# A hybrid encoder layer on one core: the second norm's scale and shift move to the transposed blocks and to the last stage's residual rows, and the inputs' low parts move to VectorE

## The chip, the cores and the metric

The kernel runs on one core of one Trainium2 chip. Time is device time in microseconds of that core. Three runs of the kernel before gave 1482.79, 1483.11 and 1485.83 us; the median, 1483.11 us, is the figure to compare with. Five engines work side by side, each through its own instructions in a fixed order: TensorE (PE), VectorE (DVE), ScalarE (ACT), GpSimd (POOL) and SyncE (SP), which here only issues DMAs. An instruction that waits holds back everything behind it on its engine.

## The reference, cut to what matters

```
h = LN(x, ln0_g, ln0_b)                      # 1024 positions x 1024 channels, float32
p = h @ w_in                                 # four mixers: S5, RWKV-7, short conv, Fourier
y = concat(y_a, y_b, y_c, y_d)
h = LN(alpha*h + y @ w_out, ln1_g, ln1_b)    # the "second norm"
f = (silu(h @ w1) * (h @ w3)) @ w2           # hidden width 2816
out = LN(alpha*h + f, ln2_g, ln2_b)          # alpha = 2**0.25
LN(x, g, b) = (x - mean) * rsqrt(var + 1e-5) * g + b
```

The result of the second norm is used twice: as the input of the two hidden products, and, times alpha, as the residual under the last norm.

## The kernel before

Positions stand in 8 tiles of 128 rows. Every matmul operand in full precision is split into a high part (a cast to fp32r, "hi") and a low part (the value less its high part, "lo"), and each product is three matmuls (`mm3`, L158 to L162). A split is one ACT cast and one subtraction on POOL or on DVE (`split_to`, L1382 to L1385).

The order of the instructions on each engine is set by a scheduler that lays the program out on a simulated clock, with the priorities that the code gives, so the program's text alone doesn't give the order. The stages that the change touches:

**The output projection** (about 640 to 800 us of the profile, beside the end of the RWKV scan at first and the start of the hidden products at last). The tiles go from 7 down to 0. For each tile:
- `residual` (L1428) loads the rows of x, recomputes the first norm from its kept mean and reciprocal deviation `st0` (DVE, L1432), multiplies by alpha times the first norm's scale (POOL, L1434) and adds alpha times its shift (DVE, L1435). The scale and shift rows are spread over the 128 partitions in the tile `rows`.
- `out_load` (L1437) loads the mixers' output `yraw` and splits it: the cast on ACT, the low part on DVE for tiles 7 and 6, on POOL for tiles 5 to 0 (the last argument in L1441).
- `out_product` (L1446) makes two halves of 24 matmuls, each in a PSUM bank `ops`; two banks of that kind (tag `pj`) take turns. DVE adds each half to the residual (L1455), which is also what gives the bank back to PE.
- `norm` (L1462) takes mean and variance (L172 to L187) and applies them with the scale and shift rows `g1`, `b1` in two DVE instructions of 128x1024 with two tensor inputs each (L1465, L1466).
- `turn` (L1507), once for every two tiles, transposes the normed rows on PE into PSUM (`ot`, L1518), copies each group of four 128x128 blocks to SBUF with one ACT copy (L1519), multiplies the rows by alpha (ACT, L1520), writes them to DRAM as `d_acc` (L1521), and makes seven sums and differences of the blocks `hb` on DVE (L1528 to L1535), each split into the hidden products' operands `H` (the products are done by a 2x2 scheme with seven products in place of eight).

**The hidden products** (`ff_hidden`, L1597) run from about 780 to 1273 us, with weights split on the way.

**The last product** (`ff_second`, L1668) has seven products n = 0 to 6 of 11 steps, about 31 us each. The left operands `fa` come back from DRAM; the right ones `fb` are made of `w2` tiles, by a sum on DVE (L1725), a cast on ACT and a low part on DVE, in a ring of six buffers, four steps ahead. Four PSUM banks are added to the rows `acc` when a product ends (L1761). After product 3 the residual rows are read back from `d_acc` through a ring of two buffers `fx` (L1779) and added on DVE (L1780). The last norm (`ff_out`, L1801) is applied by ACT, POOL and DVE with the rows `g2`, `b2` (`b2` lies in the tile `rmask`), loaded once by ACT's DMA queue at L1678 and L1679.

Of the kernel before, what the change touches and what calls it, by code (L numbers as in the profile page):

```python
# [12 lines left out]
F32 = mybir.dt.float32  # L13
# [10 lines left out]
NT = S // 128  # L24
# [12 lines left out]
for _name, _cols in (  # L37
    ("ln0_g", 8), ("ln0_b", 8), ("mu_rkv", 12), ("w0", 4), ("a0", 4), ("k_k", 2), ("k_a", 2),
    ("r_k", 2), ("gn_g", 2), ("gn_b", 2), ("conv_w", 6), ("glu_b", 2), ("mu_w", 16), ("mu_a", 16),
    ("mu_g", 8), ("lam_re", 16), ("lam_im", 16), ("log_dt", 16),  # L40
):
    VEC[_name] = (_n, _cols)
    _n += _cols
# [3 lines left out]
def pack(inp):  # L47
# [9 lines left out]
        col(a["rwkv_mu_w"][0]), col(a["rwkv_mu_a"][0]), col(a["rwkv_mu_g"][0]),  # L57
        s5(a["s5_lambda_re"]), s5(a["s5_lambda_im"]), np.repeat(a["s5_log_dt"][0], 64, axis=0),
    ], axis=1)
    rows = np.stack([a["ln0_g"], a["ln0_b"], a["ln1_g"][0], a["ln1_b"][0], a["ln2_g"][0], a["ln2_b"][0]])  # L60
# [79 lines left out]
class Trunk:  # L140
# [1264 lines left out]
    def row_load(self, out, i):  # L1405
        self.nc.scalar.dma_start(out=out, in_=self.A["rows"][i:i + 1, :].to_broadcast([128, D]))


    def out_first(self):
        nc = self.nc  # L1410
        rows = self.t("TT", [128, 4, D], "rows")
        self.row4 = [rows[:, i] for i in range(4)]
        for i in range(4):
            self.row_load(rows[:, i], i)
        for i in range(2):
            nc.scalar.mul(out=rows[:, i], in_=rows[:, i], mul=ALPHA)
        self.acc = [None] * NT
# [10 lines left out]
    def residual(self, t, tag):  # L1428
        nc = self.nc
        ht = self.acc[t] = self.t(tag, [128, D], "acc")  # L1430
        nc.sync.dma_start(out=ht, in_=self.A["x"][t * 128:(t + 1) * 128, :])
        nc.vector.tensor_scalar(out=ht, in0=ht, scalar1=self.st0[:, t, 0:1], scalar2=self.st0[:, t, 1:2],  # L1432
                                op0=ALU.subtract, op1=ALU.mult)
        nc.gpsimd.tensor_tensor(out=ht, in0=ht, in1=self.row4[0], op=ALU.mult)  # L1434
        nc.vector.tensor_tensor(out=ht, in0=ht, in1=self.row4[1], op=ALU.add)  # L1435

    def out_load(self, t):  # L1437
        nc = self.nc
        raw = self.raw("yraw").rearrange("p (k s) -> p k s", k=8)
        nc.sync.dma_start(out=raw, in_=self.d_y[:, :, t * 128:(t + 1) * 128].rearrange("k p s -> p k s"))  # L1440
        self.split_to(*self.y_parts(t), raw, nc.vector if t > 5 else None)  # L1441

# [14 lines left out]
    def out_proj(self):  # L1457
        nc = self.nc
        g1, b1 = self.row4[2:]
        self.raws = ["WR", "T7"]  # L1460

        def norm(t):  # L1462
            ht = self.acc[t]
            mean, rstd = self.row_stats(self.m, ht, D, LN_EPS)
            nc.vector.scalar_tensor_tensor(out=ht, in0=ht, scalar=mean, in1=g1, op0=ALU.subtract, op1=ALU.mult)  # L1465
            nc.vector.scalar_tensor_tensor(out=ht, in0=ht, scalar=rstd, in1=b1, op0=ALU.mult, op1=ALU.add)  # L1466

# [39 lines left out]
    def turn(self, j, tags):  # L1507
# [4 lines left out]
        for t, dst in ((7 - 2 * j, (b11, b21)), (6 - 2 * j, (b12, b22))):  # L1512
            ht = self.acc[t]
            for q in range(2):
                ps = self.ps("fs", [128, 4, 128], "ot")
                for k in range(4):
                    kt = 4 * q + k
                    nc.tensor.transpose(ps[:, k, :], ht[:, kt * 128:(kt + 1) * 128], self.ident)  # L1518
                nc.scalar.copy(out=dst[q], in_=ps)  # L1519
            nc.scalar.mul(out=ht, in_=ht, mul=ALPHA)  # L1520
            nc.sync.dma_start(out=self.d_acc[t], in_=ht)  # L1521
        H = self.H[j // 2]
# [145 lines left out]
    def ff_second(self):  # L1668
# [8 lines left out]
        self.b2 = self.rm[:, 0:D]  # L1677
        self.row_load(self.g2, 4)  # L1678
        self.row_load(self.b2, 5)  # L1679

# [81 lines left out]
        for n in range(6):  # L1762
# [13 lines left out]
            if n == 3:  # L1776
                for t in range(NT - 1, -1, -1):
                    x = self.ring("x", [128, D])
                    nc.sync.dma_start(out=x, in_=self.d_acc[t])  # L1779
                    tt(out=self.acc[t], in0=self.acc[t], in1=x, op=ALU.add)  # L1780

        fill(la, ls, P)
# [56 lines left out]
```

## Time and profile before

| | |
|---|---|
| median of three runs | 1483.11 us |
| the profiled execution, its own time | 1484.06 us |
| its span, first to last instruction | 1482.3 us |
| mean granted TensorE clock | 0.954 of full speed |
| PE busy | 1323.5 us (89% of the span) |
| DVE busy | 1097.4 us (74%) |
| ACT busy | 626.5 us (42%) |
| POOL busy | 587.8 us (40%) |

The shares are means over stages with different limits. Each stage has to be read by itself: how busy each engine is in it, and which wait of PE ends last. In a trace row, "[6.80 <-ACT H L1384]" means that the engine stood idle for 6.80 us and that, by the profile, the last thing to come was ACT's instruction of line 1384. Where an engine waits for several things, that name can be the wrong one of them, so it is checked against the time at which the named instruction ended.

### The profile page before, as it was taken

Reading aid. Unit: us, or ns where it says so; the run is one execution under the profiler, and the core shown is the slowest. Engines: PE = TensorE matmul, PEld = TensorE weight load, DVE = VectorE, ACT = ScalarE, POOL = GpSimd, SP = SyncE. Lnnn points to the kernel's source line nnn. Section 1 sums busy time; section 2 is a strip of 40 time slices with the busy share of each in tenths; the row PEclk is TensorE's granted clock in tenths of the full one; section 3 lists DMA queues with packets and bytes.
Section 4 is the critical chain, followed back from the end, with each engine's and each line's share of the span. In section 5 each row is a group of like instructions: output and inputs, shape, how many; then the busy total and the mean of one; then the engine's idle time right before and its main releaser. Section 6 shows DMA issues by size and latency. Waiting matters only on the chain.

```text
span 1482.3 us, 23747 instructions
## 1 busy us (share of the span) xinstructions
PE 1323.5 (89%) x9072; PEld 1196.4 (81%) x9072; DVE 1097.4 (74%) x1907; ACT 626.5 (42%) x1208; POOL 587.8 (40%) x530
## 2 busy tenths in 40 slices
PE   6968798977897989998976999999999999699995
PEld 5968787766796877776766999999999998588884
DVE  8997966497986775789999866666666664245886
ACT  4312151646315784751436544444444443232231
POOL 6467653162464424134648533333333330000008
PEclk9989999999898998999998999999999999899998
DMA  6111032131424014163313434334444459955852
GB/s 238 58 43 29 18 96 76 58 85 58 114 86 136 16 36 155 39 187 123 124 33 117 150 129 142 134 140 154 157 157 143 147 188 381 357 191 185 275 165 113
DMA packets 97056, 193.95 MB, mean 131 GB/s; under 512 B 24624, under 2 KB 50864, under 8 KB 96944
## 3 DMA queue, kind: packets, MB, share of 16 engines
q1 hardware_dynamic: 94912, 187.59, 37.6%
q10 hardware_dynamic: 2032, 4.86, 1.0%
q8 instruction: 71, 1.16, 0.3%
q14 instruction: 41, 0.34, 0.1%
HBM read 127.41 MB, written 63.96 MB: 129 GB/s over the span
## 4 chain that ended last, share of the span: by engine, by line
PE 41%; DVE 10%; DMA 6%; issue 2%; ACT 1%; POOL 1%; DVEq 0%; SPq 0%; ACTq 0%; POOLq 0%
PE fx L160 5%; PE fx L162 5%; PE fx L161 5%; PE f L160 4%; PE f L162 4%; PE f L161 4%; DMA fg<-w 3%; PE fy L160 2%; PE fy L162 2%; PE fy L161 2%; DVE acc L1435 1%; PE fz L160 1%; PE fz L161 1%; PE fz L162 1%; DMA d_f<-fg 1%
## 5 line engine op out<-in xcount | busy, mean ns | idle before, releaser
L160 PE MATMUL proj<-HA,wh 128*128 128x256 f32 x672 | 194.3, 289 | 14.7 <-DVE la L919 11.9
L160 PE MATMUL fx<-H,fc 128*128 128x256 f32 x704 | 197.2, 285 | 5.5 <-ACT fc L1384 2.2
L162 PE MATMUL fx<-H,fc 128*128 128x256 f32 x704 | 198.6, 284 | 2.6 <-DVE fc L1385 2.6
L161 PE MATMUL proj<-HB,wh 128*128 128x256 f32 x672 | 199.2, 296 | 1.9 <-POOL HB L334 1.9
L1385 POOL TENSOR_TENSOR fc<-fw,fc 128x512 fp32r<-128x512 f32 x96 | 137.7, 1436 | 158.9 <-ACT fc L1384 158.1
L162 PE MATMUL proj<-HA,wl 128*128 128x256 f32 x672 | 195.3, 291 | 4.4 <-POOL wl L394 4.4
L161 PE MATMUL fx<-H,fc 128*128 128x256 f32 x704 | 199.2, 283 | 0.0
L160 PEld LDWEIGHTS proj<-HA,wh 128*128 128x128 f32 x672 | 130.4, 194 | 18.5 <-DVE la L919 7.6
L160 PEld LDWEIGHTS fx<-H,fc 128*128 128x128 f32 x704 | 133.1, 191 | 7.5 <-ACT fc L1384 2.9
L162 PEld LDWEIGHTS proj<-HA,wl 128*128 128x128 f32 x672 | 130.4, 194 | 10.3 <-issue 5.5
L162 PEld LDWEIGHTS fx<-H,fc 128*128 128x128 f32 x704 | 134.5, 192 | 2.9 <-DVE fc L1385 2.8
L161 PEld LDWEIGHTS proj<-HB,wh 128*128 128x128 f32 x672 | 130.4, 194 | 7.1 <-issue 4.8
L161 PEld LDWEIGHTS fx<-H,fc 128*128 128x128 f32 x704 | 134.9, 192 | 0.1
L160 PE MATMUL f<-fb,fa 128*128 128x512 f32 x276 | 109.6, 397 | 13.0 <-DMA fa<-d_f 13.0
L162 PE MATMUL f<-fb,fa 128*128 128x512 f32 x276 | 109.3, 396 | 0.0
L161 PE MATMUL f<-fb,fa 128*128 128x512 f32 x276 | 109.2, 396 | 0.0
L1818 POOL TENSOR_TENSOR acc<-acc,g 128x1024 f32<-128x1024 f32 x7 | 17.2, 2467 | 220.2 <-ACT acc L1817 220.2
L160 PE MATMUL fy<-H,fc 128*128 128x256 f32 x352 | 100.0, 284 | 4.7 <-ACT fe L1642 3.6
L162 PE MATMUL fy<-H,fc 128*128 128x256 f32 x352 | 99.5, 284 | 0.2 <-DVE fc L1385 0.2
L161 PE MATMUL fy<-H,fc 128*128 128x256 f32 x352 | 99.5, 283 | 0.0
L1384 ACT CAST fc<-fw 128x512 fp32r<-128x512 f32 x120 | 73.8, 618 | 31.8 <-POOL fc L1385 15.7
L1385 POOL TENSOR_TENSOR fc<-fs,fc 128x512 fp32r<-128x512 f32 x24 | 34.2, 1426 | 118.7 <-ACT fc L1384 109.5
(602 smaller groups left out, 3769.3 us busy)
## 6 DMA issues: line engine op xcount, KB each, us to landing
fa<-d_f SPq DMA_DIRECT2D x77, 512.0 KB, 4.4
d_f<-fg SPq DMA_DIRECT2D x70, 512.0 KB, 2.9
fw<-w SPq DMA_DIRECT2D x48, 512.0 KB, 3.7
fg<-w SPq DMA_DIRECT2D x44, 256.0 KB, 5.8
wraw<-w_in SPq DMA_DIRECT2D x16, 512.0 KB, 3.9
xt<-x SPq DMA_DIRECT2D x8, 512.0 KB, 8.2
oraw<-w_out SPq DMA_DIRECT2D x8, 512.0 KB, 3.6
yraw<-d_y SPq DMA_DIRECT2D x8, 512.0 KB, 4.1
```

Source lines behind the costliest of these rows:

```text
L160: mm(out, whi, xhi, start=start, stop=False, skip_group_check=shared)
L161: mm(out, whi, xlo, start=False, stop=False, skip_group_check=shared)
L162: mm(out, wlo, xhi, start=False, stop=stop, skip_group_check=shared)
L1384: nc.scalar.copy(out=hi, in_=raw)
L1385: (eng or nc.gpsimd).tensor_tensor(out=lo, in0=raw, in1=hi.bitcast(F32), op=ALU.subtract)
L1435: nc.vector.tensor_tensor(out=ht, in0=ht, in1=self.row4[1], op=ALU.add)
L1818: nc.gpsimd.tensor_tensor(out=o, in0=o, in1=self.g2, op=ALU.mult)
```

## The change

Six edits, all in how the norms around the output projection are applied:

1. `norm` applies mean and reciprocal deviation alone, by one DVE instruction with two per-partition scalars, and writes these plain rows to `d_acc` at once. The two instructions with `g1` and `b1` are gone.
2. `turn` gives scale and shift while the transposed blocks leave PSUM: a channel then lies on a partition, so each 128x128 block takes one ACT instruction with a per-partition scale and bias (64 in all) in place of 16 copies of four blocks. ACT's multiplication of the rows by alpha (8 instructions) is gone. The scale and shift columns are two more entries of the table `vec`.
3. `residual`'s first step goes from DVE to ACT, with a bias `nm0` = -mean x reciprocal deviation, computed once.
4. `out_load`'s low parts of tiles 5 to 0 go from POOL to DVE.
5. In the last stage, after product 3, every tile gets DVE's addition of alpha x `ln1_b`, POOL's multiplication of the read-back row by alpha x `ln1_g`, and then the addition there was.
6. `g2` and `b2` hold these two rows first (loaded and multiplied by alpha on ACT), and are loaded again with the last norm's rows afterwards, by ACT's DMA queue.

```diff
@@ tables and rows @@
+    ("ln1_g", 8), ("ln1_b", 8),
...
+    def alpha_row(self, out, i):
+        self.row_load(out, i)
+        self.nc.scalar.mul(out=out, in_=out, mul=ALPHA)
...
+        self.nm0 = self.cp.tile([128, NT], F32, name="nm0")
+        nc.vector.scalar_tensor_tensor(out=self.nm0, in0=self.st0[:, :, 0], scalar=-1.0, in1=self.st0[:, :, 1],
+                                       op0=ALU.mult, op1=ALU.mult)
@@ residual @@
-        nc.vector.tensor_scalar(out=ht, in0=ht, scalar1=self.st0[:, t, 0:1], scalar2=self.st0[:, t, 1:2],
-                                op0=ALU.subtract, op1=ALU.mult)
+        nc.scalar.activation(out=ht, in_=ht, func=AF.Identity, scale=self.st0[:, t, 1:2], bias=self.nm0[:, t:t + 1])
@@ out_load @@
-        self.split_to(*self.y_parts(t), raw, nc.vector if t > 5 else None)
+        self.split_to(*self.y_parts(t), raw, nc.vector)
@@ norm @@
-            nc.vector.scalar_tensor_tensor(out=ht, in0=ht, scalar=mean, in1=g1, op0=ALU.subtract, op1=ALU.mult)
-            nc.vector.scalar_tensor_tensor(out=ht, in0=ht, scalar=rstd, in1=b1, op0=ALU.mult, op1=ALU.add)
+            nc.vector.tensor_scalar(out=ht, in0=ht, scalar1=mean, scalar2=rstd, op0=ALU.subtract, op1=ALU.mult)
+            nc.sync.dma_start(out=self.d_acc[t], in_=ht)
@@ turn @@
-                nc.scalar.copy(out=dst[q], in_=ps)
-            nc.scalar.mul(out=ht, in_=ht, mul=ALPHA)
-            nc.sync.dma_start(out=self.d_acc[t], in_=ht)
+                for k in range(4):
+                    nc.scalar.activation(out=dst[q][:, k], in_=ps[:, k, :], func=AF.Identity,
+                                         scale=self.v("ln1_g", 4 * q + k), bias=self.v("ln1_b", 4 * q + k))
@@ ff_second, its start @@
-        self.row_load(self.g2, 4)
-        self.row_load(self.b2, 5)
+        self.alpha_row(self.g2, 2)
+        self.alpha_row(self.b2, 3)
@@ ff_second, after product 3 @@
                     nc.sync.dma_start(out=x, in_=self.d_acc[t])
+                    tt(out=self.acc[t], in0=self.acc[t], in1=self.b2, op=ALU.add)
+                    nc.gpsimd.tensor_tensor(out=x, in0=x, in1=self.g2, op=ALU.mult)
                     tt(out=self.acc[t], in0=self.acc[t], in1=x, op=ALU.add)
+                self.row_load(self.g2, 4)
+                self.row_load(self.b2, 5)
```

The scheduler lays the changed program out anew. Three places show what that does. Line numbers of the changed kernel are larger than those of the kernel before, by 2 to 12: L1387 there is L1385 here, L1442 is L1435, L1462 is L1455, L1535 is L1528, L1769 is L1761.

The first place is DVE in the output projection, between the additions of tile 3's second half and of tile 2's first half to their residuals (the two L1455 rows around it, of which the second stands last here). The kernel before:

```order
L1435 TENSOR_TENSOR acc_6677<-acc_6677,rows_6026 128x1024
L174 BN_AGGR bnmv_6685<-bnst_6682 128x2
L1528 TENSOR_TENSOR hb_6574<-hb_6572 128x512
L1465 SCALAR_TENSOR_TENSOR acc_6554<-acc_6554,bnmv_6685,rows_6026 128x1024
L1529 TENSOR_TENSOR hb_6574<-hb_6573,hb_6574 128x512
L1532 TENSOR_TENSOR hb_6572<-hb_6573,hb_6572 128x512
L184 RECIPROCAL bnr_6687<-bnr_6687 128x1
L1385 TENSOR_TENSOR H_6274<-hb_6574,H_6274 128x512
L1535 TENSOR_TENSOR hb_6573<-hb_6573,hb_6574 128x512
L1455 TENSOR_TENSOR acc_6677<-ops_6695,acc_6677 128x512
```

The changed kernel at the same place, from the addition of tile 3's second half (first row) to that of tile 2's first half (the row of ops_6711):

```order
L1462 TENSOR_TENSOR acc_6562<-ops_6663,acc_6562 128x512
L174 BN_STATS bnst_6698<-acc_6562 128x6
L1387 TENSOR_TENSOR y_583_6278<-yraw_6763,y_582_6277 128x1024
L176 BN_AGGR bnmv_6701<-bnst_6698 128x2
L1442 TENSOR_TENSOR acc_6693<-acc_6693,rows_6026 128x1024
L1535 TENSOR_TENSOR hb_6582<-hb_6580 128x512
L1442 TENSOR_TENSOR acc_6767<-acc_6767,rows_6026 128x1024
L1462 TENSOR_TENSOR acc_6693<-ops_6711,acc_6693 128x512
L1536 TENSOR_TENSOR hb_6582<-hb_6581,hb_6582 128x512
L1539 TENSOR_TENSOR hb_6580<-hb_6581,hb_6580 128x512
```

Of the eight rows that stood between tile 2's residual addition (L1435) and the addition of its first half, only the first difference of blocks (L1528, now L1535) still does; the mean and variance now come earlier, the norm's row (L1465) is gone, and the other five follow later. A low part of `yraw` and tile 1's residual addition (the second L1442) have come ahead of it.

The second place is ACT at the same time, with the copies of the transposed blocks of tile 5's second and tile 4's first half. The kernel before:

```order
L1519 COPY hb_6573<-ot_6581 128x512
L1520 ACTIVATE acc_6357<-acc_6357 128x1024
L1384 CAST H_6273<-hb_6573 128x512
L1384 CAST y_582_6277<-yraw_6747 128x1024
L1519 COPY hb_6572<-ot_6589 128x512
L1519 COPY hb_6573<-ot_6595 128x512
L1520 ACTIVATE acc_6480<-acc_6480 128x1024
```

The changed kernel (x4 is four instructions, one for each block):

```order
L1527 ACTIVATE hb_6581<-ot_6592,vec 128x128 x4
L1386 CAST H_6273<-hb_6581 128x512
L1440 ACTIVATE acc_6693<-acc_6693,nm_6031,st_81 128x1024
L1386 CAST y_582_6277<-yraw_6763 128x1024
L1440 ACTIVATE acc_6767<-acc_6767,nm_6031,st_81 128x1024
L1527 ACTIVATE hb_6580<-ot_6601,vec 128x128 x4
L1527 ACTIVATE hb_6581<-ot_6610,vec 128x128 x4
```

Each copy has become four instructions, the alpha multiplications are gone, and the first steps of two residuals, which wait for their loads of x, stand among them.

The third place is DVE in the last product, after product 3, whose four banks are `f_1227` to `f_1230`. The kernel before:

```order
L1761 TENSOR_TENSOR acc_12226<-f_1227_12906,acc_12226 128x512 x2
L1385 TENSOR_TENSOR fb_13180<-fs_13178,fb_13180 128x512
L1761 TENSOR_TENSOR acc_12226<-f_1228_12907,acc_12226 128x512 x2
L1780 TENSOR_TENSOR acc_12226<-acc_12226,fx_13130 128x1024
L1761 TENSOR_TENSOR acc_12225<-f_1229_12908,acc_12225 128x512 x2
L1780 TENSOR_TENSOR acc_12226<-acc_12226,fx_13133 128x1024
L1761 TENSOR_TENSOR acc_12225<-f_1230_12909,acc_12225 128x512 x2
L1385 TENSOR_TENSOR fb_13198<-fs_13178,fb_13198 128x512
```

The changed kernel, where L1788 is the addition of alpha x `ln1_b` and L1790 the addition of the read-back row:

```order
L1788 TENSOR_TENSOR acc_12260<-acc_12260,rmask 128x1024
L1769 TENSOR_TENSOR acc_12259<-f_1230_12943,acc_12259 128x512 x2
L1788 TENSOR_TENSOR acc_12260<-acc_12260,rmask 128x1024
L1387 TENSOR_TENSOR fb_13250<-fs_13230,fb_13250 128x512
L1788 TENSOR_TENSOR acc_12260<-acc_12260,rmask 128x1024
L1790 TENSOR_TENSOR acc_12260<-acc_12260,fx_13164 128x1024
L1788 TENSOR_TENSOR acc_12259<-acc_12259,rmask 128x1024
L1387 TENSOR_TENSOR fb_13269<-fs_13267,fb_13269 128x512
L1788 TENSOR_TENSOR acc_12259<-acc_12259,rmask 128x1024
L1790 TENSOR_TENSOR acc_12260<-acc_12260,fx_13169 128x1024
```

The eight new additions stand between the low parts `fb` that the next product's steps need, and the additions of the read-back rows have moved back behind them.

## Rows read from the trace of the kernel before

**Rows 1.** Stages: stretch, length, busy us (x count) of each engine, PE clock, DMA
```profile
640.00:750.00 110.00, 94.51 (x481) 76.48 (x481) 103.13 (x177) 39.60 (x80) 60.38 (x35) 0.95 0.41 133
775.00:840.00 65.00, 51.06 (x356) 47.92 (x355) 59.76 (x72) 39.43 (x82) 46.67 (x30) 0.87 0.38 124
840.00:1273.00 433.00, 430.62 (x3502) 423.33 (x3501) 274.91 (x364) 195.02 (x349) 134.80 (x98) 1.00 0.50 176
1373.00:1404.00 31.00, 31.00 (x135) 25.02 (x134) 26.84 (x38) 7.11 (x12) 0.00 (x0) 1.00 0.86 287
1404.00:1435.00 31.00, 31.00 (x136) 25.16 (x135) 26.46 (x44) 11.55 (x19) 0.00 (x0) 1.00 0.61 190
```
**Rows 2.** PE's waits, 640 to 750 us: waiter, releaser, total us, times, longest
```profile
PE ops L160 <- ACT H L1384: 6.8, 1, 6.8
PE pgn L1373 <- DVE TN L1374: 3.5, 2, 2.8
PE ops L160 <- DVE acc L1455: 2.4, 3, 1.4
```
**Rows 3.** Time line: PE's longest wait, and the ACT instruction named as its releaser
```profile
748.31 0.77 PE L160 MATMUL ops<-owa,y 128*128 128x512 f32 x1 [6.80 <-ACT H L1384]
...
748.12 1.04 ACT L1384 CAST H<-yraw 128x1024 fp32r<-128x1024 f32 x1
```
**Rows 4.** Time line of DVE before that wait ended
```profile
732.49 0.68 DVE L1455 TENSOR_TENSOR acc<-ops,acc 128x512 f32<-128x512 f32 x1
...
735.54 3.46 DVE L1435 TENSOR_TENSOR acc<-acc,rows 128x1024 f32<-128x1024 f32 x1
...
741.74 2.29 DVE L1465 SCALAR_TENSOR_TENSOR acc<-acc,bnmv,rows 128x1024 f32<-128x1024 f32 x1
...
747.48 0.68 DVE L1455 TENSOR_TENSOR acc<-ops,acc 128x512 f32<-128x512 f32 x1
```
**Rows 5.** Groups, 640 to 750 us: busy us, mean ns, idle before
```profile
L1465 DVE SCALAR_TENSOR_TENSOR acc<-acc,bnmv,rows 128x1024 f32<-128x1024 f32 x5 | 9.4, 1882 | 0.0
...
L1432 DVE TENSOR_SCALAR acc<-acc,st 128x1024 f32<-128x1024 f32 x8 | 8.0, 996 | 1.5 <-DMA acc<-x 1.5
...
L1385 POOL TENSOR_TENSOR y<-yraw,y 128x1024 fp32r<-128x1024 f32 x3 | 7.7, 2579 | 1.2 <-ACT y L1384 1.2
L1466 DVE SCALAR_TENSOR_TENSOR acc<-acc,bnr,rows 128x1024 f32<-128x1024 f32 x4 | 7.6, 1905 | 0.1
...
L1385 POOL TENSOR_TENSOR H<-yraw,H 128x1024 fp32r<-128x1024 f32 x2 | 4.8, 2406 | 0.0
...
L1520 ACT ACTIVATE acc<-acc 128x1024 f32<-128x1024 f32 x4 | 4.3, 1063 | 0.0
```
**Rows 6.** Time lines: a low part on POOL, and one on DVE
```profile
735.03 2.89 POOL L1385 TENSOR_TENSOR y<-yraw,y 128x1024 fp32r<-128x1024 f32 x1
...
654.52 1.21 DVE L1385 TENSOR_TENSOR y7l<-yraw,y7h 128x1024 fp32r<-128x1024 f32 x1
```
**Rows 7.** ACT's forms: four blocks with scale and bias, a copy, a row
```profile
28.98 1.51 ACT L332 ACTIVATE hf<-n0ps,vec 128x128 f32<-128x128 f32 x4 [1.28 <-PE n0ps L322]
...
L1519 ACT COPY hb<-ot x16: 569/587/591, 697.3 to 791.6; 128x512 f32<-128x512 f32 x16
...
L1817 ACT ACTIVATE acc<-acc,bnn,bnr x7: 1229/1242/1248, 1442.7 to 1463.0; 128x1024 f32<-128x1024 f32 x7
```
**Rows 8.** PE's longest waits, 775 to 840 us
```profile
PE fy L160 <- ACT fe L1642: 3.6, 2, 2.6
PE fx L162 <- DVE fc L1385: 2.6, 1, 2.6
```
**Rows 9.** The last stage: an addition, a cast, and POOL's multiplication in the last norm
```profile
1384.17 1.23 DVE L1780 TENSOR_TENSOR acc<-acc,fx 128x1024 f32<-128x1024 f32 x1 [1.25 <-DMA fx<-d_acc]
...
1378.28 0.62 ACT L1384 CAST fb<-fs 128x512 fp32r<-128x512 f32 x1 [2.19 <-PE f L162]
...
L1818 POOL TENSOR_TENSOR acc<-acc,g x7: 2390/2412/2807, 1444.0 to 1469.9; 128x1024 f32<-128x1024 f32 x7
```
**Rows 10.** PE's wait between the hidden products and the last product
```profile
1284.71 0.80 PE L160 MATMUL f<-fb,fa 128*128 128x512 f32 x1 [12.96 <-DMA fa<-d_f]
```

More of the change, by code (lines that the diff above doesn't have):

```diff
@@ L58, in pack @@
         s5(a["s5_lambda_re"]), s5(a["s5_lambda_im"]), np.repeat(a["s5_log_dt"][0], 64, axis=0),
+        col(a["ln1_g"][0]), col(a["ln1_b"][0]),
     ], axis=1)
@@ L1411, in out_first @@
         rows = self.t("TT", [128, 4, D], "rows")
[L1412 to L1416, printed above, removed]
+        self.row2 = [rows[:, i] for i in range(2)]
+        for x, i in zip(self.row2, range(2)):
+            self.alpha_row(x, i)
+        self.nm0 = self.cp.tile([128, NT], F32, name="nm0")
+        nc.vector.scalar_tensor_tensor(out=self.nm0, in0=self.st0[:, :, 0], scalar=-1.0, in1=self.st0[:, :, 1],
+                                       op0=ALU.mult, op1=ALU.mult)
         self.acc = [None] * NT
@@ L1431, in residual @@
         nc.sync.dma_start(out=ht, in_=self.A["x"][t * 128:(t + 1) * 128, :])
-        nc.vector.tensor_scalar(out=ht, in0=ht, scalar1=self.st0[:, t, 0:1], scalar2=self.st0[:, t, 1:2],
-                                op0=ALU.subtract, op1=ALU.mult)
-        nc.gpsimd.tensor_tensor(out=ht, in0=ht, in1=self.row4[0], op=ALU.mult)
-        nc.vector.tensor_tensor(out=ht, in0=ht, in1=self.row4[1], op=ALU.add)
+        nc.scalar.activation(out=ht, in_=ht, func=AF.Identity, scale=self.st0[:, t, 1:2], bias=self.nm0[:, t:t + 1])
+        nc.gpsimd.tensor_tensor(out=ht, in0=ht, in1=self.row2[0], op=ALU.mult)
+        nc.vector.tensor_tensor(out=ht, in0=ht, in1=self.row2[1], op=ALU.add)
     def out_load(self, t):
@@ L1458, in out_proj @@
         nc = self.nc
-        g1, b1 = self.row4[2:]
         self.raws = ["WR", "T7"]
```

## The prediction

> **What bounds the kernel now.** I read the stages first, then in each the waits of PE, and only then single instructions. In the stages view [rows 1] the hidden products (840 to 1273 us) keep PE busy 430.6 of 433 us, and the last product keeps it busy without a gap (31.0 of 31.0 in both stretches shown). There only more work for PE, or a new wait, could change the time. Two stretches are different. From 640 to 750 us, the output projection, PE is busy 94.5 of 110 us and DVE 103.1; from 775 to 840 PE is busy 51.1 of 65, at a mean granted clock of 0.87 of 2.4 GHz, and DVE 59.8. So the projection is bound by DVE, which has nearly no free time, and PE's idle 15.5 us in 640 to 750 is what a lighter DVE can give back.
>
> The view of PE's waits [rows 2] says what that idle time is: one wait of 6.8 us, put down to an ACT cast, 3.5 us for a gate row of the RWKV output, and 2.4 us for the additions L1455. The long one has the wrong name beside it. The matmul starts at 748.31, and the cast named starts only at 748.12 and takes 1.04 us [rows 3], so it can't be the releaser. What ends just then is DVE's L1455, 747.48 + 0.68 = 748.16 [rows 4]: it empties one of the two `ops` banks, and PE needs that bank. The addition before it began at 732.49. For 15 us DVE worked through other rows of its queue, among them L1435 at 3.46 us and L1465 at 2.29 us. The wait is DVE's order and DVE's slowness.
>
> Why L1435 takes 3.46 us is seen beside POOL. The same kind of instruction, two tensors of 128x1024 from SBUF, takes 1.21 us at 654.52; at 735.54 it overlaps POOL's low part of 735.03 to 737.92 and ends 1.1 us after it [rows 4, 6]. DVE's work here is therefore partly standing behind POOL.
>
> **The change part by part.**
>
> *DVE in the output projection, 640 to 750 us.* Out go L1432 (8.0 us and 1.5 us of waiting for its load), five L1465 (9.4 us) and four L1466 (7.6 us): 26.5 us [rows 5]. In come four instructions with two per-partition scalars, the form of L1432 at 0.996 us each, so 4.0 us, and five of the six low parts at 1.21 us, so 6.1 us [rows 5, 6]. POOL loses the five low parts in this stretch (7.7 + 4.8 = 12.5 us). A DVE row caught behind one of them loses up to 3.46 - 1.21 = 2.25 us; I take 1.2 us for each, 6 us, since some of them ran beside rows that are already counted. DVE is relieved of 26.5 - 10.1 + 6 = 22 us out of 103, and PE, busy 94.5 us, becomes the limit.
>
> What PE gets of it I count from its waits. In the new order only one block difference and tile 1's residual addition stand between tile 2's residual addition and the bank's addition, where eight rows stood. At the least (1.21 us each for the low part, two residual additions and the difference, and two short rows) the addition comes some 6 us after the one before it; with two of them caught for 2.25 us each it is some 11, against 15 before. I take 5.5 of the 6.8 us, and of the other two waits (5.9 us), which end on rows late in the same queue, 4.5. **Gain 10 us; ends 3 and 15.5.** The lower end has the additions held by POOL's L1434, which stays, and by the loads of x; the upper is all of PE's idle time.
>
> *ACT in the output projection.* 16 copies at 0.587 us become 16 groups of four at 1.51 us: +14.8 us. Eight alpha multiplications at 1.063 us go: -8.5 us. Eight first steps of the residuals come, in L1817's form at 1.24 us: +9.9 us [rows 5, 7]. ACT gets 16 us more over 200 us; in 640 to 750 it is busy only 39.6 of 110 us [rows 1], and that free time hides it. What is queued behind a residual's step while it waits for its load of x are casts of `yraw` and transposed blocks; DVE had this wait before (1.5 us in all). 0 us.
>
> *775 to 840 us*, the last two turns and the first hidden products. DVE loses one L1465 and one L1466 for one lighter row, ACT has about seven copies and four multiplications there, so 7 x 0.92 - 4.3 = +2 us. PE's largest waits there are for ACT (3.6 us) and for DVE (2.6 us) [rows 8]. The two signs cancel: **0 us, ends -3 and +4**.
>
> *The last product.* Eight additions at 1.23 us come to DVE, 9.8 us, and eight POOL multiplications at 2.41 us [rows 9]. The first two multiplications run early, when their rows have landed; six fall beside DVE's rows and may hold them 0 to 2.25 us each, 0 to 13.5 us. DVE is busy 53.3 of the 62 us of products 4 and 5 [rows 1], so 8.7 us are free. Beyond that PE has a lead: ACT's cast waits for PE to free a buffer (2.19 us idle before it [rows 9]), so the ring of right operands is full and runs four steps of 31/11 = 2.8 us ahead, 11 us. With 1.5 us for each held row DVE owes 18.8 us against 8.7 + 11. The lead is not all to be had, since the first steps need theirs early. **Cost 3 us; ends 0 and 14.6** (9.8 + 13.5 - 8.7, with no lead). The second load of `g2` on ACT's queue waits for POOL's last multiplication, with casts behind it; its place is at the ninth of product 5's eleven casts, about 25 us ahead of the product's end, so I count nothing.
>
> *The rest.* The scaled rows cost ACT four multiplications of 1.06 us, two of which there were; `d_acc` is written earlier, and eight small columns more are loaded for each of scale and shift. The scheduler also exchanges a few rows before 640 us. 0 us, ends -2 and +2.
>
> *Is a gain hidden later?* Before the last product PE waits 12.96 us for its left operands [rows 10]. These loads follow the hidden products' last stores, so they move with them, and I expect that wait to stay as long as it is.
>
> **The sum:** -10 + 0 + 0 + 3 + 0 = -7 us on the profiled execution's 1484.06 us (span 1482.3 us), 1477.06. That execution lies 0.95 us over the median of the runs shown, so 1476.1 us: I predict 1476.
>
> **The rivals.**
>
> *The last product becomes bound by DVE.* Place: products 4 and 5. Price: all six multiplications hold a DVE row for the full 2.25 us and no lead is left, 14.6 us against the gain of 10: +4.6 us, so 1487.7. It decides from the point where DVE's debt is larger than 8.7 + 11 us. For it: L1435's 3.46 us beside POOL, and the additions' place ahead of the low parts. Against it: the lead, and that DVE's additions from PSUM take 0.68 us [rows 4] in a stretch where POOL is busy too. The Trainium skill, "SBUF — State Buffer", section "Who interferes with whom", says that a DVE instruction with two SBUF inputs contends with a GpSimd one that reads SBUF, and that the one that starts first holds the other until it ends. By that rule a row could stand for the whole 2.41 us, 14.5 us for the six, and the time would be 1488.7; the rows agree with the kind of wait (3.46 against 1.21 us).
>
> *All of the relief reaches PE and the end costs nothing:* -15.5 and -2 more in 775 to 840, so 1465.6. For it: 22 us off DVE is more than PE's idle time. Against it: POOL's L1434 and the block sums stay.
>
> *ACT becomes late in 775 to 840.* Its in-order queue holds the casts of the first hidden products behind the groups of four; it costs the upper end, 4 us, and with half the gain (5 us) and the end's 3 us that is +2 us, so 1485.1; with the full gain 1480.1. The middle is 1482.6. For it: PE already waits there on ACT. Against it: ACT is busy 39.4 of 65 us.
>
> **How the numbers follow.** Forecast 1476: 0.52, with its own range 1471 to 1481. All relief, 1466: 0.14. ACT late, 1482.6: 0.19. Last product bound, 1488: 0.15. Within 0.2% of 1483.11 (1480.1 to 1486.1) is about what a measurement of this kernel can't tell from no change. Faster: 0.46 of the first case, 0.14, 0.04 of the third, 0.64. Same: 0.06, 0.14 and 0.03 of the last, 0.23. Slower: 0.01 and 0.12, 0.13. The range has to reach to the middles of the cheap and the dear case: 1466 to 1487.
>
> **What would show it.** DVE's busy time in the projection should fall by about 20 us, L1442 should still show up to 3.5 us beside POOL's L1441, and the wait of 6.8 us should be 0 to 3 us; the hidden products should start about 10 us earlier, with the later stages shifted alike. In products 4 and 5 PE should show one or two waits on `fb`, 3 us in all. The forecast is wrong if PE's idle time in the projection is still over 12 us, or if the waits in the last product pass 8 us.

## The result and the profile after

The changed kernel took 1497.71 us (median of five runs, 1495.89 to 1498.56), against 1482.79 us for the kernel before in the same comparison: a ratio of 1.0096, 95% interval 1.0082 to 1.0111. It is slower by 14.9 us in the medians, 14.2 us by the ratio, where I had forecast 7 us faster. The profiled execution took 1498.14 us, its span 1496.1 us, 13.8 us more than before.

A stage table finds the place of a loss faster than any list of groups. I take six marks that both programs have: the first matmul of `pre` (the RWKV stage begins), of `ops` (the output projection), the first and last of `fx` (the hidden products), the first matmul of the last product after its wait for `fa`, and POOL's first multiplication of the last norm. They are the first and last starts that the view of one tile gives, and the table shows the time between them, in us.

| | to `pre` | `pre` to `ops` | `ops` to `fx` | `fx` first to last | to last product | to last norm | to the end | median |
|---|---|---|---|---|---|---|---|---|
| before | 275.1 | 379.6 | 119.6 | 465.0 | 45.4 | 159.3 | 38.3 | 1482.79 |
| after | 280.3 | 377.9 | 115.6 | 468.5 | 46.1 | 169.6 | 38.1 | 1497.71 |
| difference | +5.2 | -1.7 | -4.0 | +3.5 | +0.7 | +10.3 | -0.2 | |
| e1 | 281.4 | 378.6 | 122.0 | 465.7 | 48.1 | 159.7 | 38.4 | 1492.82 |
| e2 | 275.7 | 377.7 | 121.0 | 466.7 | 47.4 | 169.0 | 38.2 | 1497.53 |
| e3 | 279.4 | 374.7 | 115.0 | 466.9 | 46.9 | 160.6 | 38.4 | 1486.82 |
| e4 | 280.9 | 375.5 | 114.8 | 467.8 | 45.3 | 160.7 | 38.4 | 1486.06 |
| e5 | 274.5 | 377.8 | 115.2 | 467.4 | 45.7 | 170.3 | 38.2 | 1491.05 |
| e6 | 274.0 | 377.8 | 114.3 | 466.9 | 45.8 | 159.4 | 38.3 | 1481.32 |
| e7 | 280.0 | 375.2 | 114.9 | 467.5 | 46.0 | 164.3 | 38.2 | 1488.64 |
| e8 | 279.5 | 375.3 | 114.8 | 468.4 | 46.0 | 162.5 | 38.3 | 1488.38 |
| e9 | 274.6 | 377.6 | 115.3 | 465.4 | 46.4 | 159.8 | 42.1 | 1478.65 |
| e10 | 274.6 | 376.8 | 123.4 | 466.7 | 46.0 | 160.6 | 38.3 | 1488.25 |
| e11 | 274.7 | 377.4 | 116.9 | 463.2 | 46.1 | 160.3 | 38.6 | 1478.44 |
| e12 | 280.3 | 374.9 | 114.8 | 468.1 | 47.4 | 171.1 | 38.1 | 1496.79 |

Each row is one profiled execution; `pre` to `ops`, which no experiment aims at, differs by 4.9 us among them, so a difference of 2 us in one cell says little. Five profiles that have `nm0` as early as the changed kernel (e3, e4, e7, e8, e12) took 374.7 to 375.5 us there; between 520 and 600 us their granted clock was 0.94 (e4, e12), and 0.89 in the changed kernel's profile. So 2 to 3 us that the changed kernel's profile loses by `ops` are not in theirs, and their medians lie 2 to 4 us lower than the last stage alone would put them; no run isolates why. The losses are +5.2 us before 275 us, +3.5 us in the hidden products, and +10.3 us in the last stage; the gain is 4.0 us in the projection. Projection and hidden products together took 584.1 us against 584.6, so the hidden products take back nearly all that the projection gains. The rows of the stages of [rows 1], now for the changed kernel (stretch, length, busy us and count of PE, PEld, DVE, ACT, POOL, granted clock, DMA share, GB/s):

```profile
640.00:750.00 110.00, 101.85 (x525) 83.91 (x524) 93.58 (x182) 55.54 (x116) 45.45 (x32) 0.95 0.43 135
775.00:840.00 65.00, 53.95 (x399) 51.30 (x398) 59.87 (x71) 43.19 (x101) 46.47 (x30) 0.92 0.30 100
840.00:1273.00 433.00, 427.08 (x3450) 419.86 (x3450) 272.27 (x364) 192.45 (x344) 132.33 (x96) 0.99 0.48 173
1373.00:1404.00 31.00, 30.27 (x131) 24.10 (x129) 26.44 (x32) 4.33 (x7) 8.02 (x2) 1.00 0.70 235
1404.00:1435.00 31.00, 29.68 (x121) 23.98 (x122) 31.00 (x39) 7.83 (x13) 10.99 (x4) 0.94 0.73 254
```

In the projection PE's idle time fell from 15.5 to 8.2 us, and DVE's busy time from 103.1 to 93.6. In the last row DVE has no free time left: 31.00 of 31 us, against 26.46.

**The early loss.** It lies where the change does nothing but add one DVE row of 0.15 us, `nm0`, at 45 us. The scheduler's simulated clock moved with it, and from DVE's 117th row on the S5 stage came out in another order. DVE's time line before, around the row `la` that PE's next projections wait for:

```profile
160.63 0.68 DVE L919 TENSOR_TENSOR la<-proj,lb 128x512 f32<-128x512 f32 x1
161.23 2.74 DVE L793 TENSOR_TENSOR_SCAN s5xw<-s5tt,s5x 64x1024 f32<-64x1024 f32 x1
164.00 2.97 DVE L795 TENSOR_TENSOR_SCAN s5xw<-s5tt,s5x 64x1024 f32<-64x1024 f32 x1
```

And in the changed kernel (L919 is now L921):

```profile
159.62 2.28 DVE L795 TENSOR_TENSOR_SCAN s5xw<-s5tt,s5x 64x1024 f32<-64x1024 f32 x1
161.93 3.17 DVE L797 TENSOR_TENSOR_SCAN s5xw<-s5tt,s5x 64x1024 f32<-64x1024 f32 x1
...
168.29 0.68 DVE L921 TENSOR_TENSOR la<-proj,lb 128x512 f32<-128x512 f32 x1
```

The second pair of scans now stands ahead of `la`, not behind it, and `la` comes 7.7 us later. In the view of PE's waits from 100 to 260 us, before and then after, the same wait grows by 7.7 us:

```profile
PE proj L160 <- DVE la L919: 11.9, 3, 6.8
```
```profile
PE proj L162 <- DVE la L921: 19.6, 2, 14.5
```

The granted clock falls with it, 0.90 before and 0.76 after between 140 and 175 us. The stages rows of that stretch, before and then after:

```profile
140.00:175.00 35.00, 26.05 (x204) 25.27 (x203) 33.79 (x29) 4.28 (x6) 24.73 (x20) 0.90 0.12 18
```
```profile
140.00:175.00 35.00, 19.64 (x151) 19.27 (x150) 33.36 (x26) 3.64 (x4) 25.82 (x19) 0.76 0.13 17
```

**The projection.** The wait of 6.8 us [rows 2] is gone, and smaller ones stand in its place: 6.4 us in three waits on DVE's additions. The time lines of the changed kernel, ACT and DVE ahead of one of them, and PE:

```profile
734.39 1.24 ACT L1440 ACTIVATE acc<-acc,nm,st 128x1024 f32<-128x1024 f32 x1 [3.77 <-DMA acc<-x]
735.54 1.03 ACT L1386 CAST y<-yraw 128x1024 fp32r<-128x1024 f32 x1
...
736.60 2.59 DVE L1387 TENSOR_TENSOR y<-yraw,y 128x1024 fp32r<-128x1024 f32 x1 [2.69 <-ACT y L1386]
...
744.28 0.68 DVE L1462 TENSOR_TENSOR acc<-ops,acc 128x512 f32<-128x512 f32 x1
...
745.11 0.47 PE L162 MATMUL ops<-owa,y 128*128 128x512 f32 x1 [1.69 <-DVE acc L1462]
760.58 0.70 PE L162 MATMUL ops<-owa,H 128*128 128x512 f32 x1 [3.38 <-DVE acc L1462]
```

Edits 3 and 4 together made a chain: ACT stands 3.77 us for the load of x, the cast of `yraw` stands behind it, and the low part, which was POOL's, now keeps DVE idle for 2.69 us. That low part is itself held, 2.59 us in place of 1.21, while POOL runs its L1441.

What POOL's relief did for DVE is seen in the view of one line, the residual's last addition (least, median and greatest ns of eight), before and after:

```profile
L1435 DVE TENSOR_TENSOR acc<-acc,rows x8: 1211/2970/3460, 667.5 to 748.1; 128x1024 f32<-128x1024 f32 x8
```
```profile
L1442 DVE TENSOR_TENSOR acc<-acc,rows x8: 1164/1212/1219, 676.7 to 743.1; 128x1024 f32<-128x1024 f32 x8
```

None of these is held any more, though L1441 on POOL stayed; I had expected rows of up to 3.5 us still.

**The hidden products** start as early as before (773.8 us), but PE has one new wait. Rows of three engines from the changed kernel's time line:

```profile
849.21 0.69 DVE L1582 TENSOR_TENSOR fs<-fw 128x512 f32<-128x512 f32 x1 [0.96 <-DMA fw<-w]
849.82 0.42 DVE L1665 TENSOR_TENSOR fg<-fe,fe 128x256 f32<-128x256 f32 x1
850.33 0.40 ACT L1386 CAST fg<-fg 128x256 fp32r<-128x256 f32 x1 [1.76 <-DVE fg L1665]
850.64 0.58 ACT L1646 COPY fe<-fx 128x512 f32<-128x512 f32 x1
851.27 0.58 PE L162 MATMUL fx<-H,fc 128*128 128x256 f32 x1 [4.38 <-ACT fe L1646]
```

ACT's copy, which empties PE's bank, stands behind a cast that waits for DVE, and DVE waited for a load. A stretch at the lower of the two clock levels follows: PE's granted clock is 0.63 from 851 to 858 us, so 0.94 from 840 to 900, where it was 1.00.

**The last stage.** Rows of POOL, DVE, ACT and PE behind product 3, from the changed kernel's time line:

```profile
1394.35 8.02 POOL L1789 TENSOR_TENSOR fx<-fx,g 128x1024 f32<-128x1024 f32 x2 [93.35 <-DMA fx<-d_acc]
...
1395.36 1.21 DVE L1788 TENSOR_TENSOR acc<-acc,rmask 128x1024 f32<-128x1024 f32 x1
1396.49 1.28 DVE L1733 TENSOR_TENSOR fs<-fg,fg 128x512 f32<-128x512 f32 x2
...
1397.28 1.22 ACT L1386 CAST fb<-fs 128x512 fp32r<-128x512 f32 x2 [11.00 <-DVE fs L1733]
...
1400.06 3.40 DVE L1790 TENSOR_TENSOR acc<-acc,fx 128x1024 f32<-128x1024 f32 x1 [1.69 <-POOL fx L1789]
...
1404.59 1.28 DVE L1387 TENSOR_TENSOR fb<-fs,fb 128x512 fp32r<-128x512 f32 x2
...
1405.32 0.50 PE L163 MATMUL f<-fb,fa 128*128 128x512 f32 x1 [2.05 <-DVE fb L1387]
```

All eight additions L1788 run between 1380.9 and 1396.6 us, ahead of the sums `fs` that the next steps need; ACT has nothing to cast for 11 us. Then DVE waits 1.69 us for POOL, and its row takes 3.40 us in place of 1.23 [rows 9] beside POOL's second multiplication. The wait works both ways: the first of POOL's two multiplications in the row above took 5.68 us beside DVE's rows, where 2.4 us is usual. PE loses only 2.05 us and some time at the lower clock; its last matmul comes 187.1 us after the stage's first, against 182.3. The rest appears later. The chain that ended last, before:

```profile
1467.46 0.70 DVE acc L1761
1468.19 0.70 DVE bnst L172
1469.16 4.07 DVE acc L1809 x2
1474.09 1.89 DVE acc L1811
```

and after:

```profile
1457.99 1.11 POOL acc L1830
...
1469.86 4.72 POOL acc L1830 x2
1474.58 2.32 POOL acc L1831
...
1490.18 2.29 POOL acc L1831
```

Before, the end hung on PE's last matmul and DVE's last rows. Now it hangs on POOL's fourteen operations of the last norm, which follow each other without a gap from the first. They did so before as well, and ended at 1478.18 us, only 0.55 us ahead of DVE's last row (1478.73), so POOL's chain had next to no slack to begin with. Its first and last rows, and DVE's last, in the kernel before:

```profile
1443.98 4.79 POOL L1818 TENSOR_TENSOR acc<-acc,g 128x1024 f32<-128x1024 f32 x2 [220.25 <-ACT acc L1817]
...
1472.65 5.53 POOL L1819 TENSOR_TENSOR acc<-acc,rmask 128x1024 f32<-128x1024 f32 x2
...
1474.09 4.64 DVE L1811 SCALAR_TENSOR_TENSOR acc<-acc,bnr,rmask 128x512 f32<-128x512 f32 x2
```

The chain starts with the norm of the first tiles, whose statistics DVE reaches, in the changed kernel, only when it is nearly done with product 6's operands. Before, DVE had worked off its queue and stood waiting for product 5's end. DVE's first rows of these statistics behind product 5 (one half row is taken earlier in both), before, with the addition ahead of them, and then after; against the stage's first matmul they come 10.9 us later:

```profile
1434.62 1.40 DVE L1761 TENSOR_TENSOR acc<-f,acc 128x512 f32<-128x512 f32 x2 [2.52 <-PE f L162]
1435.94 1.28 DVE L172 BATCH_NORM_STATS2 bnst<-acc 128x6 f32<-128x512 f32 x2
```
```profile
1450.54 1.86 DVE L174 BATCH_NORM_STATS2 bnst<-acc 128x6 f32<-128x512 f32 x3
```

### The profile page after: what moved, and what is told of

It is laid out like the page before. It is cut to its first block, busy times and chain, and to the rows that moved or that the text cites. A ratio compares the mean times of both kernels' runs of the same rounds, so it can differ in the third digit from the quotient of the medians.

```text
span 1496.1 us, 23819 instructions
## 1 busy us (share of the span) xinstructions
PE 1333.3 (89%) x9072; PEld 1206.1 (81%) x9072; DVE 1093.3 (73%) x1906; ACT 644.5 (43%) x1258; POOL 588.3 (39%) x532
## 4 chain that ended last, share of the span: by engine, by line
PE 35%; DVE 11%; DMA 7%; POOL 3%; ACT 2%; issue 2%; POOLq 0%; SPq 0%; DVEq 0%; ACTq 0%
PE fx L162 4%; PE fx L163 4%; PE fx L164 4%; DMA fg<-w 3%; PE fy L162 2%; PE f L162 2%; PE fy L163 2%; PE fy L164 2%; PE f L163 2%; PE f L164 2%; DMA fw<-w 1%; PE ops L162 1%; PE ops L163 1%; PE ops L164 1%; DMA d_f<-fg 1%
## 5 line engine op out<-in xcount | busy, mean ns | idle before, releaser
L1387 POOL TENSOR_TENSOR fc<-fw,fc 128x512 fp32r<-128x512 f32 x96 | 136.6, 1425 | 170.9 <-ACT fc L1386 169.5
L162 PE MATMUL f<-fb,fa 128*128 128x512 f32 x276 | 106.8, 400 | 13.6 <-DMA fa<-d_f 13.6
L1789 POOL TENSOR_TENSOR fx<-fx,g 128x1024 f32<-128x1024 f32 x8 | 23.8, 2980 | 176.8 <-DMA fx<-d_acc 106.2
L1387 POOL TENSOR_TENSOR fc<-fs,fc 128x512 fp32r<-128x512 f32 x24 | 32.6, 1359 | 119.2 <-ACT fc L1386 119.2
```

The source lines that it names most:

```text
L162: mm(out, whi, xhi, start=start, stop=False, skip_group_check=shared)
L1387: (eng or nc.gpsimd).tensor_tensor(out=lo, in0=raw, in1=hi.bitcast(F32), op=ALU.subtract)
L1789: nc.gpsimd.tensor_tensor(out=x, in0=x, in1=self.g2, op=ALU.mult)
```

## The experiments

The kernel before had medians of 1483.27, 1483.12, 1483.40 and 1482.28 us in the four comparisons (e1 to e4, e5 to e8, e9 to e11, e12).

**e1, edit 3 alone.** The kernel before with `nm0` and the residual's first step on ACT.

```diff
+        self.nm0 = self.cp.tile([128, NT], F32, name="nm0")
-        nc.vector.tensor_scalar(out=ht, in0=ht, scalar1=self.st0[:, t, 0:1], ...
+        nc.scalar.activation(out=ht, in_=ht, func=AF.Identity, scale=self.st0[:, t, 1:2], bias=self.nm0[:, t:t + 1])
```

> The kernel before with edit 3 alone (the residual's first step on ACT, with the bias nm0 computed once on DVE). Theory A: nm0 is one more DVE instruction at about 45 us of the span, and the scheduler then lays the S5 stage out otherwise (DVE from its 117th row on, as in the changed kernel); this costs 5 to 6 us between 140 and 260 us that nothing later gives back. With 1 to 3 us gained from eight DVE rows of 1 us that leave the output projection: 1485 to 1488 us, and the last matmul of the second S5 product (tile s5pt) 5 us later than before. Theory B: the early shift is slack and is absorbed before the output projection; then the time is 1480 to 1483 us.

1492.82 us, ratio 1.0061 (1.0044 to 1.0077). The early loss is there in full (+6.3 us to `pre`) and nothing gives it back. The size was missed, by 5 us over theory A's range: the projection was 2.4 us longer, not shorter, so edit 3 alone, with the norm's two rows still on DVE, gains nothing there.

**e2, edit 3 undone in the changed kernel.**

```diff
-        nc.scalar.activation(out=ht, in_=ht, func=AF.Identity, scale=self.st0[:, t, 1:2], bias=self.nm0[:, t:t + 1])
+        nc.vector.tensor_scalar(out=ht, in0=ht, scalar1=self.st0[:, t, 0:1], ...
```

> The changed kernel with edit 3 undone (the residual's first step on DVE again, no nm0). Theory A: the order before the output projection is the old one again and 5 to 6 us come back, less 1 to 3 us for the eight DVE rows in the projection: 1493 to 1495 us; what is left over the kernel before, 10 to 12 us, is the last stage. Theory B (the early shift is absorbed): 1498 to 1500 us.

1497.53 us, ratio 1.0088 (1.0073 to 1.0102). By its time alone, which is just under theory B's range and above theory A's, this speaks for theory B, but the stages say otherwise: 4.6 us come back to `pre` and are still there at `ops` (653.4 against 658.2 us; against the five profiles named above, 654.1 to 656.4, only 0.7 to 3.0 us are), and the projection then takes 5.4 us more. I had allowed 1 to 3.

**e3, no scale and shift in the last stage.**

```diff
-                    tt(out=self.acc[t], in0=self.acc[t], in1=self.b2, op=ALU.add)
-                    nc.gpsimd.tensor_tensor(out=x, in0=x, in1=self.g2, op=ALU.mult)
```

> The changed kernel without the last stage's scale and shift: DVE's eight additions of b2 and POOL's eight multiplications are left out, and g2, b2 are loaded once with the last norm's rows. The output then lacks the residual's scale and shift. Theory A: the last stage owes its 10.3 us to DVE's debt in products 4 and 5 (PE's wait of 2.0 us, 3 us of low clock behind it, and POOL's chain of fourteen operations in the last norm, which starts 10 us later against the first matmul of the stage): 1486 to 1488 us. Theory B: only the wait and the low clock in the product come from there, and the late start of POOL's chain from the second load of g2: 1486 to 1488 as well, but the chain's start is then tied to the load's landing; in e4 it would not move. Theory C: the tail is late for a reason of its own (the order of the last norm): 1491 to 1493 us.

1486.82 us, ratio 1.0020 (1.0004 to 1.0035): 9.0 of the 10.3 us come back, and POOL's chain starts at 160.6 us after the stage's first matmul. Theory C falls, and so does B: the second load of g2 was issued at 1427.4 us in the changed kernel, 30 us before POOL's first row, and took 5.6 us to land, and that row waited for ACT.

**e4, the same block two products earlier.**

```diff
-            if n == 3:
+            if n == 1:
```

> The changed kernel with the block of edit 5 (the reads of d_acc, the additions of b2, POOL's multiplications, the additions of the rows, the second loads of g2 and b2) after product 1 in place of product 3. Nothing is left out. Theory A: the debt is a question of the place. From 1290 to 1373 us DVE is busy 41.6 of 83 us, enough for 8 additions more of 1.2 us, 8 of the rows and 13 us of holding by POOL; the last stage costs 0 to 2 us instead of 10.3: 1487 to 1490 us. Theory B: POOL holds DVE's rows wherever they stand and PE waits there too, 5 us or more: 1492 us or more.

1486.06 us, ratio 1.0024 (1.0011 to 1.0037). Nothing is left out, and the stage takes 160.7 us. DVE has the room there: from 1310 to 1370 us it was busy 33.1 of 60 us before. The same rows cost 10.3 us in one place and 1.4 in another.

**e5, `nm0` late.** It lies in a part of the tile `rows`, which is given out only after the RWKV stage.

```diff
-        self.nm0 = self.cp.tile([128, NT], F32, name="nm0")
+        self.nm0 = rows[:, 2, 0:NT]
```

> The changed kernel with nm0 kept in a free part of the tile rows, which is only given out when the RWKV stage has left it, so that the one small DVE instruction comes after the S5 stage; the order on DVE and POOL is then that of the kernel before up to the output projection. All else as in the changed kernel. Theory A (the early loss is the order of the S5 stage): 1491.5 to 1493.5 us, and the first matmul of the tile pre at 275 to 276 us in place of 280.3. Theory B (it is something else that the changed kernel does early, its 16 more columns of vec or a slower granted clock): 1496 to 1498 us.

1491.05 us, ratio 1.0053 (1.0041 to 1.0066), a little under theory A's range: the early loss is gone (274.5 us to `pre`), though the small instruction is still there. PE's wait of the S5 stage has its old length; the row from e5's waits:

```profile
PE proj L162 <- DVE la L921: 11.7, 2, 6.8
```

The 16 more columns of `vec` are in e5 too, so they cost nothing.

**e6, `nm0` late and the block after product 1.**

> e5 and e4 together: nm0 late, and the last stage's block after product 1. Theory A: both losses go, and what is left is the projection's gain of some 4 us less 1 to 3 us at the start of the hidden products: 1480 to 1483 us, about what the kernel before takes or a little less. Theory B (the projection's gain doesn't survive, because the stages in between absorb it): 1484 to 1487 us.

1481.32 us, ratio 0.9991 (0.9981 to 1.0001). Both losses are gone; by its interval it can't be told from the kernel before. POOL's first rows of the last norm, in e6, come 159.4 us after the stage's first matmul, as before:

```profile
1438.16 4.78 POOL L1830 TENSOR_TENSOR acc<-acc,g 128x1024 f32<-128x1024 f32 x2 [95.98 <-ACT acc L1829]
```

**e7, without DVE's additions L1788** (the shift is left out), and **e8, without POOL's multiplications L1789** (the scale is left out).

```diff
-                    tt(out=self.acc[t], in0=self.acc[t], in1=self.b2, op=ALU.add)
```

> The changed kernel without the eight additions of b2 on DVE in the last stage (the output lacks the shift of the residual); POOL's multiplications stay. Theory A (DVE's rows are the debt): the 9.8 us leave DVE's queue ahead of the sums fs that the next casts need, and the last stage gives back 6 to 10 of its 10.3 us: 1488 to 1492 us. Theory B (POOL's holding and lateness is the debt): 0 to 4 us come back: 1493.5 to 1498 us.

```diff
-                    nc.gpsimd.tensor_tensor(out=x, in0=x, in1=self.g2, op=ALU.mult)
```

> The changed kernel without POOL's eight multiplications in the last stage (the output lacks the scale of the residual); DVE's additions of b2 stay, and g2 isn't loaded with the first scale any more than before. Theory A (DVE's rows are the debt): DVE loses only its wait for POOL of 1.7 us and some held rows, 2 to 5 us: 1492.5 to 1496 us. Theory B (POOL is the debt): 7 to 10 us come back: 1487.5 to 1490.5 us.

1488.64 us (ratio 1.0042, 1.0029 to 1.0055) and 1488.38 us (1.0044, 1.0031 to 1.0057). The stage takes 164.3 and 162.5 us, so either alone gives back 5.3 and 7.1 of the 10.3 us. Their sum is more than the whole, which fits a debt that counts only above what an engine has free. The count doesn't come out in full: with some 9.8 us of rows or some 9.9 us of holding and waiting against 8.7 us free, either would have left about 1 us, and 5.0 and 3.2 us were left; why is open. In neither profile does PE wait for an operand after the stage's first matmul, so this loss doesn't show in PE's waits. Neither theory was right by itself; e7 met theory A's time, with a little less than its 6 to 10 us in the stage, and e8 met theory B's numbers. (In e8 `g2` is still loaded with the first scale and then again; only the multiplications are out.)

**e9, e6 with edit 4 undone** (low parts on POOL again).

```diff
-        self.split_to(*self.y_parts(t), raw, nc.vector)
+        self.split_to(*self.y_parts(t), raw, nc.vector if t > 5 else None)
```

> e6 with edit 4 undone: the low parts of tiles 5 to 0 on POOL again. Theory A (DVE's own rows bind the projection): DVE is 7 us lighter and POOL 15 us heavier, and the stretch from the first matmul of ops to the first of fx, 114.3 us in e6 and 119.6 before, stays within 2 us: 1479 to 1483 us. Theory B (DVE stands behind POOL there): the stretch goes back to 118 to 120 us and the time to 1484.5 to 1487 us.

1478.65 us, ratio 0.9966 (0.9952 to 0.9979): the only version here with nothing left out whose interval lies below 1. The projection takes 115.3 us with the low parts on POOL and 114.3 with them on DVE: edit 4 buys nothing there that one profile could tell. Where the 2.7 us between the medians of e6 and e9 come from, the profile doesn't show: its hidden products are 1.5 us shorter and its projection 1.0 us longer. Most of the additions L1442 run free in e9 as well; its row has one of 3.47 us and a median of 1.22 us, so what had held them before was not the low parts alone. (e9's profile is its slowest run, 1483.79 us.)

```profile
L1442 DVE TENSOR_TENSOR acc<-acc,rows x8: 1210/1216/3468, 670.5 to 741.5; 128x1024 f32<-128x1024 f32 x8
```

**e10, e6 with edit 3 undone.**

> e6 with edit 3 undone: the residual's first step on DVE, no nm0. Theory A (eight DVE rows of 1 us decide, as e2's stretch of 121.0 us says): ops to fx 119 to 121.5 us, 1486 to 1489 us. Theory B (e2's long stretch was a matter of that one profile): 114 to 116 us, 1481 to 1483 us.

1488.25 us, ratio 1.0031 (1.0019 to 1.0043), projection 123.4 us. With e1 and e2: neither edits 1 and 2 (the norm's lighter row) nor edit 3 (the residual's step on ACT) shortens the projection alone; only both do. Each of these programs has an order of its own, so how much of this is the eight rows and how much the order isn't separated.

**e11, e6 with plain copies of four blocks** (the hidden products' input lacks scale and shift).

```diff
-                for k in range(4):
-                    nc.scalar.activation(out=dst[q][:, k], in_=ps[:, k, :], func=AF.Identity, ...
+                nc.scalar.copy(out=dst[q], in_=ps)
```

> e6 with the 64 block instructions with scale and bias replaced by the 16 plain copies of four blocks that stood there before (the hidden products' input then lacks scale and shift). ACT is 14.8 us lighter. Theory A (the heavier copies make the start of the hidden products late): fx first to last goes from 466.9 back to 465 us or less and the wait of 4.4 us for ACT's L1646 goes: 1477 to 1479.5 us. Theory B (that wait is an order of DVE rows, ACT waiting for fg): 1480 to 1482 us.

1478.44 us, ratio 0.9960 (0.9946 to 0.9974). The hidden products take 463.2 us in place of 466.9, and the 4.4 us wait is gone, as theory A has it; but the projection took 2.6 us more than in e6, so the two together are only 1.1 us shorter. And in e9, with all 64 block instructions, that wait is gone too (its largest wait on L1646 is 0.7 us; it has another of 5.6 us for DVE at 802 us). So the order has a part in whether this wait comes. How much of the 3 us is ACT's weight alone stays open.

**e12, right operands up to six steps ahead.**

```diff
-                fill(ra, rs, 4)
+                fill(ra, rs, 6)
```

> The changed kernel with the right operands of the last product made up to six steps ahead in place of four (the ring has six buffers; nothing is left out). It asks what PE's lead is worth there. Theory A (DVE's debt is hidden from PE by a lead but not paid: it comes back as a late last norm): PE's wait of 2.0 us at 1405 shrinks, yet POOL's first multiplication of the last norm still comes 166 us or more after the first matmul of the last product (169.6 in the changed kernel, 159.3 before): 1494 to 1498 us. Theory B (the wait and the low clock behind it are the loss, as the prediction's working has it): 164 us or less, 1489 to 1492.5 us.

1496.79 us, ratio 1.0090 (1.0066 to 1.0114). PE's wait only moves, from 1405 to 1424 us, and POOL's chain still starts at 171.1 us. Theory A holds: a longer lead hides DVE's debt from PE for longer and pays none of it.

## Why the prediction was wrong

*The last product* was the step that failed most: "DVE owes 18.8 us against 8.7 + 11", cost 3 us. It cost 10.3 (e3, e4). Two things were wrong in it. I counted PE's lead of 11 us as cover, but a lead only delays the time at which PE sees the debt (e12), and in e7 and e8 PE never sees it while the stage is still 5.0 and 3.2 us longer; DVE still has to do the rows, and DVE's free time was the only cover. And I looked for the price at PE alone. PE did lose little, 4.8 us; the end hung on POOL's fourteen operations, which wait for the first norm, which stands at the end of DVE's queue, and which had 0.55 us of slack before. Without the lead the working gives 18.8 - 8.7 = 10.1 us, so the price of the held rows was about right, 9 us: four rows, not six, were held beside POOL, at 1400, 1407, 1410 and 1425 us, for 1.6 to 2.2 us each, 8.2 us in all, and DVE's wait for POOL is 1.69 us more. L1790's 3.40 us ends 1.1 us after POOL's row ends (1402.37 us). The rival "the last product becomes bound by DVE" had the place, but its deciding point again counted the 11 us, and its 1487.7 (1488 among the chances, while the range ends at 1487) was still 10 us short. The rule of the Trainium skill, "SBUF — State Buffer", section "Who interferes with whom", has the right kind of wait by these rows: the trace shows DVE's rows held beside POOL's and POOL's first held beside DVE's, but four held DVE rows in place of six.

*The rest, "0 us, ends -2 and +2"*, failed for a reason that I had in front of me: I had written that the scheduler exchanges a few rows before 640 us and gave that no price. One instruction of 0.15 us, in another part of the program, cost 5.2 us through the order (e1, e5). An order that changes in a stage where PE is waiting for DVE has to be followed row by row, even where the change doesn't touch that stage.

*The projection* was right in its mechanism and too large: gain 4.0 us where I said 10, above the lower end of 3. The wait of 6.8 us went and the additions came early, but waits of 6.4 us on DVE's additions stayed. Part of the reason may be that edits 3 and 4 put DVE behind ACT's wait for x, which I had costed at nothing because DVE "had this wait before". Before, the load held only DVE's own queue; now it holds ACT's cast and through it DVE. That this chain cost the missing 6 us is not shown: e9 takes DVE's low parts out of it, and its projection is no shorter. Of the parts, the norm's lighter row and the residual's step on ACT make the gain together (114.3 to 116.9 us with both, 119.6 to 123.4 with one or none), and the low parts, which the working had at 6.1 us of DVE rows against 6 us of relief from POOL, add nothing that can be measured (e9).

*775 to 840 us*: 0 us, ends -3 and +4; the hidden products came out 3.5 us longer, inside the bounds, with one new wait of 4.4 us of the kind that the rival "ACT becomes late" describes, just behind the stretch I had named (851 us), and with DVE in front of ACT. The projection's gain is nearly all spent there: the two stages together are 0.5 us shorter in the changed kernel's profile, and 1.4 to 4.5 us in those of e3 to e9, e11 and e12.

*The wait for `fa`* moved with the hidden products as expected: 13.6 us against 12.96.

Between the forecast of -7 us and the profile's +13.8 lie 20.8 us: 7.3 from the last product, 6.0 from the projection, 5.2 from the order before `pre`, 3.5 from the hidden products, less 1.2 elsewhere.

Of the signs that I named, DVE's relief (9.6 us, not 20) and the hidden products' start (0.5 us earlier, not 10) spoke against the forecast at once; PE's waits in the last product (2.0 us, forecast 3) looked as if it had come true, and were the wrong thing to look at. Neither of the two signs that were to show the forecast wrong appeared, PE's idle time in the projection (8.2 us, not over 12) and the waits in the last product (2.0 us, not over 8): both watched PE, and the loss ran past it.

## What to carry to other kernels

In this kernel a lead hid an engine's debt but did not pay it (e12): count the free time of the engine that gets new rows up to the end of its queue, ask what stands last there, and put work that has no due time into the stage where that engine is idle (e4: the same rows, 9 us cheaper two products earlier). Where a scheduler writes the order, compare the order in every stage, not only in the edited one, and pin a small new instruction to the place where it is used (e5). Undo parts one by one on a base in which the accidents are removed: on such a base the change without its low parts was worth 5 us (e9: 3 to 7 by its interval).

## What the runs showed that I had not expected

The last norm's time from POOL's first row to the end of the kernel was 38.1 to 38.6 us in every profile but one, whatever came before. In e9's, 42.1 us, DVE's two halves of L1821 took 8.93 us beside POOL, where they took 4.07 in the kernel before. That explains a part: DVE's last row ended 36.3 us after POOL's first, against 34.7 before, and the other 2 us lie behind DVE's last row, unexplained. The row of e9's time line:

```profile
1464.24 8.93 DVE L1821 SCALAR_TENSOR_TENSOR acc<-acc,bnmv,g 128x512 f32<-128x512 f32 x2
```
